# One adaLN row by ScalarE and accumulating transfers, and the sums over later keys as products of high and low parts

## The chip, the cores and the metric

One Trainium2 chip, one of its NeuronCores. The time is device microseconds of one execution of the whole kernel, as the median of several runs; lower is better. The engines are PE (TensorE, the matrix unit; PEld is its loading of weights), DVE (VectorE), ACT (ScalarE), POOL (GpSimd, which also issues transfers) and SP (SyncE, which issues transfers only). Each engine works through its own list of instructions in order; semaphores hold an instruction until what it needs is there.

## The reference

One layer of a decoder, in float32: batch 1, 512 positions, width 2048. The part that the change touches:

```python
c_act = jax.nn.silu(c)
mod = c_act @ w_ada[layer] + b_ada[layer]          # 2048 x 12288
sh1, sc1, gt1, sh2, sc2, gt2 = jnp.split(mod[:, None, :], 6, axis=-1)
h = rmsnorm(x, g_mix[layer]) * (1 + sc1) + sh1
x = x + (1 + gt1) * mixer(h, positions, w_in[layer], w_a[layer], w_b[layer], w_o[layer])
...
# stick-breaking attention, 8 heads of 128, in blocks of 128 queries
z = jnp.einsum('bqhd,bkhd->bhqk', q_blk, k) * scale
log1m = jnp.where(past, -jax.nn.softplus(z), 0.0)
after = lax.cumsum(log1m, axis=3, reverse=True) - log1m
w = jnp.where(past, jnp.exp(jax.nn.log_sigmoid(z) + after), 0.0)
```

`gt1`, the mixing gate's row, is a product of one vector with a 2048 x 2048 part of `w_ada`. `after` is, for each query and key, the sum of `log1m` over the later keys. The mixer has a second group of 8 heads, sparse ones, whose keys are chosen by an indexer: 16 small heads score every key, and the 256 best stay.

## The kernel before, in words

**High and low parts.** Most products take float32 operands as two fp32r numbers each, a high part (a copy by ACT, L168) and a low part (the difference, by DVE, L170), and three matmuls: high by high, high by low, low by high (`mm3`, L178 to L180). PE takes such a matmul in one pass. Products with plain f32 operands are exact and take two passes.

**Stages.** Up to 190 us: the norm, the first adaLN rows, queries of the indexer. From 190 to 800 us 31 calls of `unit`, each a pair of 128-column blocks of the input projection; beside each one the function `between` is called twice, and each call moves a piece of other work one step on (`work`: rope tables, the indexer's ropes, the shift's values) and may do one adaLN product. From 829 to 877 us the index loop: PE makes the dots (L905), ACT the relu (L907), DVE weighs and adds them (L912), three blocks for each of 16 index heads; ropes are split before by L896 and L897. Then the eight stick-breaking heads (to about 985 us), beside which DVE picks the best 256 of the scores (L932, L933); the eight sparse heads (to 1115 us); the projections `w_b` and `w_o`; the up-projection (1400 to 2240 us) and the down-projection.

**Fills.** `values(0)` and `values(1)` project the values of the sparse heads, 32 steps of six matmuls of 512 columns each (L178 to L180 on banks `att`). The index loop and the heads call `run(fill, n)` to set such steps between their own work, so that PE has something to do while a score goes through ACT and DVE. The order in which an engine at last has its instructions is not the order of the code: a scheduler sets it when the kernel is built.

**A stick-breaking head.** `stick_1`: scale q (L964), the scores z (L971, L972), absolute value, exp, ln (L975 to L978, ACT). `stick_2`: the softplus, masked (L985, DVE), and sums of its strips, `a` and `b` (L989 to L991). `stick_3`: nine products with a triangle or with ones add the sums over later keys onto z in PSUM (L1003), then exp (L1007). `stick_4`: the weights by the values (L1013), one head late.

**The adaLN rows.** The six rows of `mod` are 96 tiles of 128 numbers. For `w_ada` lying transposed, one number is the dot of a row of the tile with c. Such a tile is two halves of 128 x 1024: a load of 512 KB (`ada_load`, L576 and the loop above) and one instruction of DVE that multiplies and adds up along the row (L585, `some_ada`), which ends in a read of its sum. Tiles 32 to 79, 96 halves, are spread over the units, the index loop, the stick-breaking and the sparse heads; `ada_end(32, 48)` finishes the mixing gate's tiles, and `ts` adds 1. The last gate's row is made otherwise, beside the up-projection: ACT scales 128 x 1024 of `w_ada` by c (L1397), and a transfer adds the product to a DRAM tile (L1398).

**Transfers.** `fetch`, `save` and `queries` issue on POOL (L838, L875), `load` and `ada_load` on SP. A transfer with `accum_op` adds to what lies in DRAM.

## Time and profile before

| | us |
|---|---|
| median of 3 runs | 2684.82 |
| fastest and slowest of them | 2680.04, 2685.26 |
| the profiled execution | 2685.6 |
| its span | 2683.8 |
| adaLN products on DVE (L585, 91 recorded) | 109.4 |
| index loop (first L886 to first scores, L971) | 829.3 to 876.5 |
| first L1003 of heads 0, 1, ..., 7 | 883.63, 897.14, ..., 974.00 |

The span runs from the first to the last instruction of the profiled execution, all else of its time lies around it. In a row of the timeline stand the start, the duration, the engine, the line and operation, what is written from what, and its shape; a row with x8 is eight instructions that follow each other, and its duration is that of the group. In brackets stands how long the engine was idle before it, and what it waited for. A matmul's duration holds its latency too, so that its price in a sequence is the distance from its start to the next start. The DMA share is the mean busy share of the 16 DMA engines.

### The profile page before, as it was taken

Reading aid. Unit: us, or ns where it says so; the run is one execution under the profiler, and the core shown is the slowest. Engines: PE = TensorE matmul, PEld = TensorE weight load, DVE = VectorE, ACT = ScalarE, POOL = GpSimd, SP = SyncE. Lnnn points to the kernel's source line nnn. Section 1 sums busy time; section 2 is a strip of 40 time slices with the busy share of each in tenths; the row PEclk is TensorE's granted clock in tenths of the full one; section 3 lists DMA queues with packets and bytes.
Section 4 is the critical chain, followed back from the end, with each engine's and each line's share of the span. In section 5 each row is a group of like instructions: output and inputs, shape, how many; then the busy total and the mean of one; then the engine's idle time right before and its main releaser. Section 6 shows DMA issues by size and latency. Waiting matters only on the chain.

```text
span 2683.8 us, 47520 instructions
## 1 busy us (share of the span) xinstructions
PE 2653.4 (99%) x18644; PEld 2430.8 (91%) x18644; DVE 2396.1 (89%) x3395; ACT 1436.1 (54%) x2031; POOL 322.6 (12%) x526
## 2 busy tenths in 40 slices
PE   8999999999999999999999999999999999999998
PEld 6779999999997778889999999999999998887877
DVE  8979989999988999889888999999999997888887
ACT  4445455554446665435565555555555555546443
POOL 0010011000012211112220000000000001003121
PEclk9999999999999999999999999999999999999999
DMA  9984565566676638856763366666666646559775
GB/s 352 346 298 138 174 212 189 189 204 227 205 218 224 223 127 281 298 183 207 233 201 108 128 186 188 185 181 181 178 185 177 183 137 236 166 164 246 213 227 150
DMA packets 166157, 546.40 MB, mean 204 GB/s; under 512 B 21718, under 2 KB 22358, under 8 KB 165932
## 3 DMA queue, kind: packets, MB, share of 16 engines
q1 hardware_dynamic: 117804, 402.72, 45.6%
q0 software_dynamic: 47536, 140.26, 18.8%
q8 instruction: 146, 2.39, 0.3%
q14 instruction: 79, 0.65, 0.1%
q10 hardware_dynamic: 592, 0.39, 0.0%
HBM read 451.35 MB, written 88.52 MB: 201 GB/s over the span
## 4 chain that ended last, share of the span: by engine, by line
PE 87%; DVE 5%; DMA 3%; issue 2%; ACT 2%; POOL 0%; SPq 0%; ACTq 0%; POOLq 0%; DVEq 0%
PE att L179 14%; PE att L178 14%; PE att L180 14%; PE acc L179 13%; PE acc L180 13%; PE acc L178 12%; DVE wl L170 1%; DMA raw<-in_w_qi 1%; PE acc L1003 1%; DMA sumd<-F 1%; PE outs L179 1%; PE outs L178 1%; PE outs L180 1%; PE outs L1110 1%; ACT wh L168 1%
## 5 line engine op out<-in xcount | busy, mean ns | idle before, releaser
L168 ACT ACTIVATE wh<-raw 128x1024 fp32r<-128x1024 f32 (+2 forms) x783 | 822.3, 1056 | 936.2 <-DVE raw L295 188.4
L170 DVE TENSOR_TENSOR wl<-raw,wh 128x1024 fp32r<-128x1024 f32 (+2 forms) x783 | 945.0, 1214 | 121.0 <-ACT wh L168 113.8
L178 PE MATMUL acc<-F,wh 128*128 128x256 f32 (+3 forms) x2427 | 692.4, 286 | 1.8 <-ACT F L512 1.1
L180 PE MATMUL acc<-F,wl 128*128 128x256 f32 (+3 forms) x2427 | 690.0, 284 | 2.8 <-DVE wl L170 2.7
L179 PE MATMUL acc<-F,wh 128*128 128x256 f32 (+3 forms) x2427 | 689.8, 284 | 0.3 <-DVE F L540 0.3
L178 PE MATMUL att<-F,wh 128*128 128x256 f32 (+2 forms) x2420 | 688.8, 285 | 0.1
L180 PE MATMUL att<-F,wl 128*128 128x256 f32 (+2 forms) x2420 | 687.2, 284 | 0.0
L179 PE MATMUL att<-F,wh 128*128 128x256 f32 (+2 forms) x2420 | 686.6, 284 | 0.2 <-DVE F L199 0.2
L178 PEld LDWEIGHTS acc<-F,wh 128*128 128x128 f32 (+1 forms) x2427 | 454.8, 187 | 14.1 <-ACT wh L168 3.6
L180 PEld LDWEIGHTS acc<-F,wl 128*128 128x128 f32 (+1 forms) x2427 | 454.8, 187 | 11.1 <-DVE wl L170 4.1
L179 PEld LDWEIGHTS acc<-F,wh 128*128 128x128 f32 (+1 forms) x2427 | 455.0, 188 | 8.0 <-DVE F L540 0.5
L178 PEld LDWEIGHTS att<-F,wh 128*128 128x128 f32 x2420 | 454.3, 188 | 8.3 <-ACT wh L168 1.7
L179 PEld LDWEIGHTS att<-F,wh 128*128 128x128 f32 x2420 | 454.4, 188 | 6.3 <-DVE F L199 0.7
L180 PEld LDWEIGHTS att<-F,wl 128*128 128x128 f32 x2420 | 454.3, 188 | 6.2 <-DVE wl L170 0.6
L178 PE MATMUL att<-wh,F 128*128 128x512 f32 x448 | 178.9, 400 | 0.2 <-ACT wh L168 0.2
L179 PE MATMUL att<-wl,F 128*128 128x512 f32 x448 | 175.0, 391 | 0.0
L180 PE MATMUL att<-wh,F 128*128 128x512 f32 x448 | 174.6, 390 | 0.0
L179 PE MATMUL acc<-wl,F 128*128 128x512 f32 x288 | 114.2, 397 | 2.7 <-DVE wl L170 2.7
L178 PE MATMUL acc<-wh,F 128*128 128x512 f32 x288 | 113.0, 394 | 2.3 <-ACT wh L168 2.3
L180 PE MATMUL acc<-wh,F 128*128 128x512 f32 x288 | 111.9, 393 | 0.0
L585 DVE SCALAR_TENSOR_TENSOR raw<-raw,raw 128x1024 f32<-128x1024 f32 x91 | 109.4, 1217 | 0.0
L178 PEld LDWEIGHTS att<-wh,F 128*128 128x128 f32 x448 | 84.3, 188 | 20.2 <-issue 2.0
(404 smaller groups left out, 3773.2 us busy)
## 6 DMA issues: line engine op xcount, KB each, us to landing
raw<-in_w_up SPq DMA_DIRECT2D x164, 512.0 KB, 3.6
raw<-in_w_ada SPq DMA_DIRECT2D x154, 512.0 KB, 5.5
raw<-in_w_x SPq DMA_DIRECT2D x128, 512.0 KB, 4.4
raw<-in_w_down SPq DMA_DIRECT2D x98, 512.0 KB, 4.4
xd<-F POOLq DMA_DIRECT2D x64, 256.0 KB, 2.9
F<-xd POOLq DMA_DIRECT2D x64, 256.0 KB, 4.6
raw<-in_w_o SPq DMA_DIRECT2D x32, 512.0 KB, 4.4
soft<-in_w_gate SPq DMA_DIRECT2D x32, 512.0 KB, 3.7
```

Source lines behind the costliest of these rows:

```text
L168: pins["wh"] = act(wh, raw, AF.Copy)
L170: pins["wl"] = tt(wl, raw, wh.bitcast(F32), ALU.subtract)
L178: mm(ps, ah, bh, start=first, stop=False, skip_group_check=not check)
L179: mm(ps, ah, bl, start=False, stop=False, skip_group_check=not check)
L180: return mm(ps, al, bh, start=False, stop=last, skip_group_check=not check)
L585: stt(w, w, 1.0, cb[half], ALU.mult, ALU.mult, accum_out=macc[:, t, half : half + 1])
L1003: mm(o, negtri if tri else negones, i, start=False, stop=True, skip_group_check=True)
L1110: mm(o[:, b * P : (b + 1) * P], vs[kb][:, hd % 4 * HD : (hd % 4 + 1) * HD], pT[b][:, kb * P : (kb + 1) * P], start=kb == 0, stop=kb == b)
```

## The change

Three parts. **First**, the row of the mixing gate, `mod[:, 32:48]`. It leaves `ada_left`, so 32 of 96 products on DVE go. A generator `mix_gate` makes it instead: 64 times SP loads 128 x 512 of `w_mix`, the gate's part of `w_ada` as it lies, ACT multiplies it with a column of c, and POOL issues a transfer that adds it to one of four DRAM tiles `mix0` to `mix3`. Four rounds fold the 128 rows of each of these to 64, 32, 16 and 8 by a load of the upper half and an accumulating store onto the lower one, four of each a round; at last one matmul with a 0/1 matrix `pick` adds up the remaining rows and puts the 2048 numbers where `mod` has them. One step of the generator runs with each call of `between`, eight in the index loop, two with each stick-breaking head until it ends.

**Second**, in the stick-breaking heads, the softplus is split into a high part (three copies on ACT) and a low part (three subtractions on DVE). Seven of the nine products of `stick_3`, those on the softplus itself, become two fp32r matmuls each, high and low, with fp32r copies of the triangle and of ones (`exact`). The two products on `a` and `b` stay f32.

**Third**, the fills and the remaining adaLN products are spread anew: the index loop takes 24 steps of `fill` in place of 32, what is left goes to the heads, and adaLN products stand only beside the units and the sparse heads.

```diff
--- before.py
+++ after.py
@@ -561,7 +561,7 @@
         save(qid[j][:, LATE], o[:, LATE])
 
 
-    ada_left = [(t, half) for half in range(2) for t in range(32, 80)]
+    ada_left = [(t, half) for half in range(2) for t in range(48, 80)]
     cb[1] = None
 
     ada_ready = []
@@ -802,6 +802,45 @@
                 ada_soft.append((w, t, half))
             yield
 
+    mix_sum = [dr.tile([P, S], F32, tag=f"mix{b}", name=f"mix{b}") for b in range(4)]
+
+    def mix_gate():
+
+        ahead = None
+        for n in range(4 * KT + 1):
+            if ahead:
+                k, b, w = ahead
+                act(w, w, AF.Copy, scale=c_col[:, k : k + 1])
+                save(mix_sum[b], w, **({"accum_op": ALU.add} if k else {}))
+            if n < 4 * KT:
+                k, b = divmod(n, 4)
+                w = slot()
+                nc.sync.dma_start(w, A["w_mix"][k, :, b * S : (b + 1) * S])
+                ahead = k, b, w
+            yield
+        for rows in (64, 32, 16, 8):
+            parts_ = []
+            for s in mix_sum:
+                t = slot()[:, : 4 * rows]
+                save(t, s[rows : 2 * rows].rearrange("r (h c) -> (r h) c", c=4 * rows))
+                parts_.append(t)
+            yield
+            for s, t in zip(mix_sum, parts_):
+                save(s[:rows].rearrange("r (h c) -> (r h) c", c=4 * rows), t, accum_op=ALU.add)
+            yield
+        x, pick = slot()[:, :P], slot()[:, :KT]
+        save(pick, A["pick"])
+        for b, s in enumerate(mix_sum):
+            save(x[32 * b : 32 * b + 32], s[:8].rearrange("r (j f) -> (r j) f", f=P))
+        yield
+        yield
+        ps = outs()
+        mm(ps[:, :KT], x, pick, start=True, stop=True)
+        stt(mod[:, 32:48], ps[:, :KT], 1.0, b_ada[:, 32:48], ALU.add, ALU.add)
+        yield
+
+    mix = mix_gate()
+    next(mix)
     shift = shift_values()
 
     def beside():
@@ -818,6 +857,7 @@
                 ada_load()
             with behind(*pins):
                 next(work)
+                next(mix)
                 if i:
                     some_ada()
 
@@ -945,14 +985,10 @@
     run(index)
     fill = values(0, vb[0])
     for i in range(16):
-        run(fill, 2)
-        last = run(index, 2 if i == 15 else 1)
+        run(fill, 1 if i % 2 else 2)
+        run(index, 2 if i == 15 else 1)
         if i % 2:
-            with behind(*([last] if last else [])):
-                some_ada(len(ada_ready))
-        else:
-            ada_load()
-    run(fill)
+            run(mix)
 
 
     with behind(sig):
@@ -989,18 +1025,26 @@
         tt(a, two[:, P:], one, ALU.add)
         tt(b[:, :P], three[:, P : 2 * P], two[:, :P], ALU.add)
         tt(b[:, P:], three[:, 2 * P :], a, ALU.add)
-        return (a, b), last
+        hi = t2k("ta", 2, F32R), t2k("ta", 2, F32R), t2k("sp", 2, F32R)[:, : 2 * P]
+        lo = slot(F32R), slot(F32R), slot(F32R)[:, : 2 * P]
+        for n in (1, 2, 0):
+            sp = of_soft(soft)[n]
+            act(hi[n], sp, AF.Copy)
+            last = tt(lo[n], sp, hi[n].bitcast(F32), ALU.subtract)
+        return (a, b, strips(*hi), strips(*lo)), last
 
     def stick_3(zs, soft, later):
-        a, b = later
-        one, two, three, four = strips(*of_soft(soft))
+        a, b, hi, lo = later
+        one, two, three, four = zip(hi, lo)
         z1, z2, z3, z4 = strips(*zs)
         for o, i, tri in (
-            (z3, three, True), (z1, one, True), (z3[:, P : 2 * P], two[:, :P], False), (z3[:, 2 * P :], a, False),
+            (z3, three, True), (z1, one, True), (z3[:, P : 2 * P], cols(two, 0), False), (z3[:, 2 * P :], (a,), False),
             (z2, two, True), (z2[:, P:], one, False),
-            (z4, four, True), (z4[:, P : 2 * P], three[:, :P], False), (z4[:, 2 * P :], b, False),
+            (z4, four, True), (z4[:, P : 2 * P], cols(three, 0), False), (z4[:, 2 * P :], (b,), False),
         ):
-            mm(o, negtri if tri else negones, i, start=False, stop=True, skip_group_check=True)
+            w = negtri if tri else negones
+            for t in i:
+                mm(o, exact[:, tri * P : tri * P + P] if len(i) > 1 else w, t, start=False, stop=True, skip_group_check=True)
         w = t2k("w", 2), t2k("w", 2), t2k("sp", 2)
         for n in (1, 2, 0):
             W = (S, S, 2 * P)[n]
@@ -1017,9 +1061,15 @@
             save(yad[hd], ya[hd])
             ya[hd] = None
 
+    exact = slot(F32R)[:, : 2 * P]
+    act(exact, const[:, 2:4].rearrange("p a c -> p (a c)"), AF.Copy)
+    def both_values(first=fill):
+        yield from first
+        yield from values(1, vb[1])
+
     yad = dram("yad", 4)
     ya = [None] * NH
-    fill = values(1, vb[1])
+    fill = both_values()
     va = [fetch(vd[b]) for b in range(NQB)]
     before = None
     fetched = {}
@@ -1038,7 +1088,6 @@
 
     td = dram("td", KT)
     for hd in range(NH):
-        ada_load((3, 3, 2, 2, 3, 0, 0, 0)[hd])
         state = stick_1(hd)
         if hd + 1 < NH:
             pairs.append([fetch(xd[2 * hd + 2]), fetch(xd[2 * hd + 3])])
@@ -1046,17 +1095,17 @@
             stick_4(*before, va)
             if hd % 4 == 0:
                 va = [fetch(vd[hd + b]) for b in range(NQB)]
-        run(fill, 1 if hd < 4 else 2)
+        run(fill, 2)
+        run(mix, 2)
         if hd == NH - 1:
             cosT, sinT = (fetch(rope_d[0][:, i * S : (i + 1) * S]) for i in range(2))
             fetch_pair(0)
             for i in range(4):
                 ya[i] = fetch(yad[i])
         later, last = stick_2(*state)
-        run(fill)
+        run(fill, 1 if hd < 4 else 2)
         with behind(last):
             run(index, 3)
-            some_ada(len(ada_ready))
         before = hd, stick_3(*state, later)
         run(fill)
     run(index, 100)
@@ -1139,20 +1188,18 @@
         run(fill)
         with behind(last):
             some_ada(2 if hd > 1 else 0)
-        ada_load(2 if hd else 0)
+        ada_load()
         last = sparse_2(p, s)
         run(fill)
-        if hd > 5:
-            ada_load(3)
+        if hd > 3:
+            ada_load()
         before = hd, sparse_3(p), vb[hd // 4]
         with behind(last):
-            some_ada((2 if hd else 0) + (3 if hd > 5 else 0))
+            some_ada(2 if hd > 3 else 1)
         run(fill, 2)
     y[:3] = [split(o) for o in y[:3]]
     sparse_4(*before, y)
     run(fill)
-    ada_end(32, 48)
-    ts(mod[:, 32:48], mod[:, 32:48], 1.0, None, ALU.add)
 
 
     y[3:] = [split(o) for o in y[3:]]
@@ -1752,6 +1799,9 @@
     ada = i["w_ada"][0]
     a["w_ada"] = asc(ada[:, : 5 * D].T)
     a["w_gate"] = asc(ada[:, 5 * D :]).reshape(KT, P, D)
+    a["w_mix"] = asc(ada[:, 2 * D : 3 * D]).reshape(KT, P, D)
+    q, j = np.arange(P)[:, None], np.arange(KT)[None, :]
+    a["pick"] = asc(((q // 32 == j // 4) & (q % 4 == j % 4)).astype(np.float32))
     a["b_gate"] = asc(i["b_ada"][0][5 * D :]).reshape(1, D)
     a["c_col"] = asc(i["c"][0].reshape(KT, P).T)
 
```

PE has 18287 rows in the change and 18222 before, DVE 3173 and 3183, ACT 2079 and 1990, POOL 632 and 531, SP 854 and 822. Lines after the change have other numbers: L905 is L945, L907 is L947, L964 is L1000, L971 is L1007, L1003 is L1047, L1013 is L1057, L838 is L878, L875 is L915.

PE before, stick-breaking head 1, from its last scores on: L971 and L972 are scores and mask, L1013 the weights of head 0 by values, L178 to L180 a fill, L1003 the sums of head 1.

```order
L971 MATMUL acc_9730<-F_9623,F_9625 128x512
L972 LDWEIGHTS mask_71
L972 MATMUL acc_9730<-mask_77,mask_71 128x128
L1013 MATMUL outs_9751<-w_9710,F_9577 128x384
L1013 MATMUL outs_9751<-sp_9711,F_9579 128x256
L1013 MATMUL outs_9751<-w_9709,F_9575 128x512
L178 MATMUL att_9627<-wh_79,F_1152 128x512
L179 MATMUL att_9627<-wl_83,F_1152 128x512
L180 MATMUL att_9627<-wh_79,F_1153 128x512
```

Two more such triples follow, for banks att_9628 and att_9629, and then the sums. In the change the same place reads (L1007 and L1008 scores and mask, L1057 weights by values, L1047 the sums; `ta` and `sp` are high parts, F_10011 a low part, F_9779 the copies `exact`):

```order
L1007 MATMUL acc_9952<-F_9827,F_9829 128x512
L1008 LDWEIGHTS mask_71
L1008 MATMUL acc_9952<-mask_77,mask_71 128x128
L1057 MATMUL outs_9973<-w_9940,F_9791 128x128
L1057 MATMUL outs_9973<-w_9940,F_9787 128x384
L1057 MATMUL outs_9973<-sp_9941,F_9789 128x256
L1057 MATMUL outs_9973<-w_9939,F_9785 128x512
L1047 MATMUL acc_9953<-ta_10008,F_9779 128x384
L1047 MATMUL acc_9954<-sp_10009,F_9779 128x256
L1047 MATMUL acc_9952<-ta_10007,F_9779 128x512
L1047 MATMUL acc_9953<-F_10011,F_9779 128x384
```

The nine fill matmuls between the weights by values and the sums have gone from head 1; they stand earlier or later. In head 0 seven stand where there were 20, and from head 2 on 18 or 24 stand in this place.

POOL before, at the index loop: L875 loads the queries of index heads, two at a time, from `index`; L838 loads head 0's q and k (xd_1609, xd_1610).

```order
L875 DMA F_9187<-index_1900 128x384
L875 DMA F_9262<-index_1901 128x384
L875 DMA F_9337<-index_1902 128x384
L875 DMA F_9412<-index_1903 128x384
L838 DMA F_9567<-xd_1609 128x512
L838 DMA F_9569<-xd_1610 128x512
```

POOL in the change, from the load of the last pair of index heads' queries back to the fold before it and on to head 0's q: L825 is a fold's load, L829 its accumulating store, on tiles mix_1905 to mix_1908; L915 loads queries, L878 head 0's q.

```order
L829 DMA mix_1905<-F_9540 128x128
L829 DMA mix_1906<-F_9542 128x128
L829 DMA mix_1907<-F_9544 128x128
L829 DMA mix_1908<-F_9546 128x128
L915 DMA F_9630<-index_1903 128x384
L825 DMA F_9684<-mix_1905 128x64
L825 DMA F_9686<-mix_1906 128x64
L825 DMA F_9688<-mix_1907 128x64
L825 DMA F_9690<-mix_1908 128x64
L829 DMA mix_1905<-F_9684 128x64
L829 DMA mix_1906<-F_9686 128x64
L878 DMA F_9775<-xd_1609 128x512
```

Loads that stood next to each other now stand behind folds of the row, which wait for the folds before them.

ACT in the change, in the index loop: L936 splits queries, L947 is the relu, L1065 makes `exact`, L1000 scales head 0's q.

```order
L947 ACTIVATE w_9531<-acc_9528 128x384
L936 ACTIVATE F_9728<-F_9630 64x384
L936 ACTIVATE F_9731<-F_9630 64x384
L947 ACTIVATE w_9537<-acc_9534 128x512
L947 ACTIVATE w_9569<-acc_9566 128x256
L1065 ACTIVATE F_9779<-const 128x256
L947 ACTIVATE w_9575<-acc_9572 128x384
L947 ACTIVATE w_9581<-acc_9578 128x512
L1000 ACTIVATE F_9775<-F_9775 128x512
L947 ACTIVATE w_9599<-acc_9596 128x256
```

The scaling of q, which needs POOL's last row above, stands behind the relus of nine of the sixteen index heads and ahead of the others.

## Prediction

> **What bounds the kernel now.** I read the page from the top: span, busy shares, then the chain.
>
> ```profile
> span 2683.8 us, 47520 instructions
> PE 2653.4 (99%) x18644; PEld 2430.8 (91%) x18644; DVE 2396.1 (89%) x3395; ACT 1436.1 (54%) x2031; POOL 322.6 (12%) x526
> PE 87%; DVE 5%; DMA 3%; issue 2%; ACT 2%; POOL 0%; SPq 0%; ACTq 0%; POOLq 0%; DVEq 0%
> ```
>
> PE is busy 99% of the span and carries 87% of the chain, so a matmul that goes is worth its column time wherever PE is the limit. VectorE's 89% is a mean over stages. The windows view splits it (busy us of PE, PEld, DVE, ACT, POOL with instruction counts; granted clock; DMA share; GB/s): the units, the index loop, the stick-breaking heads, the sparse heads, the up-projection.
>
> ```profile
> 190.00:800.00 610.00, 609.24 (x5244) 602.56 (x5243) 564.99 (x728) 314.28 (x423) 55.28 (x97) 1.00 0.60 192
> 829.30:876.50 47.20, 46.81 (x212) 35.17 (x212) 44.00 (x77) 33.55 (x68) 5.90 (x11) 1.00 0.60 199
> 883.00:990.00 107.00, 106.69 (x476) 75.91 (x474) 100.72 (x240) 66.07 (x99) 19.38 (x36) 1.00 0.56 190
> 1030.00:1115.00 85.00, 85.00 (x444) 70.55 (x443) 78.40 (x170) 41.20 (x87) 14.49 (x27) 1.00 0.84 293
> 1400.00:2240.00 840.00, 839.98 (x7213) 829.56 (x7213) 783.00 (x960) 481.98 (x632) 56.71 (x85) 1.00 0.59 170
> ```
>
> PE has no gap in the units and in the up-projection. In the index loop VectorE is at 44.0 of 47.2 us, and PE's matmuls wait for what it frees. In the heads VectorE is at 94%.
>
> **The products of the sums: -7.3 us of PE.** The timeline of PE in head 5 (start, duration, line) gives every price by start-to-start.
>
> ```profile
> 946.10 0.39 PE L179 MATMUL att<-wl,F 128*128 128x512 f32 x1
> 946.32 0.39 PE L180 MATMUL att<-wh,F 128*128 128x512 f32 x1
> 946.55 1.25 PE L1003 MATMUL acc<-soft,const 128*128 128x384 f32 x6
> 947.64 0.39 PE L1003 MATMUL acc<-T,const 128*128 128x128 f32 x2
> 947.86 1.90 PE L1003 MATMUL acc<-soft,const 128*128 128x256 f32 x8
> 949.60 0.60 PE L1003 MATMUL acc<-T,const 128*128 128x256 f32 x2
> 949.84 0.58 PE L178 MATMUL att<-wh,F 128*128 128x512 f32 x1
> 950.26 0.40 PE L179 MATMUL att<-wl,F 128*128 128x512 f32 x1
> ```
>
> A high/low (fp32r) matmul of 512 columns takes 0.227 us (946.32 to 946.55); in the up-projection 839.98 / 7213 = 0.116 us is the mean of mostly 256 columns. An exact f32 product has two rows, two passes: two of 128 columns take 947.64 to 947.86, 0.11 each; the other rows resolve into 0.217, 0.322 and 0.43 a pass for 256, 384 and 512. The seven products on the softplus are four of 128 columns and one each of 384, 256 and 512. As a high and a low matmul the last three cost 2 x 0.17, 2 x 0.113 (three quarters and half of 0.227) and 2 x 0.227 instead of 2 x 0.322, 2 x 0.217, 2 x 0.43: 0.30 + 0.21 + 0.40 = 0.91 us a head, **7.3** for eight. For fp32r at 128 columns no row exists. One end is 0.057, a quarter of 0.227 (4 x 2 x 0.053 = 0.42 a head, 3.4 in all, so 10.7); the other is 0.116, a whole one of 256 (0.4 lost, so 6.9). I take 0.11, the exact pass, since loading 128 columns of weights comes with either.
>
> The Trainium skill, "TensorE: Matmul & The Clock Gate", section Back-to-back issue gap, gives about 81 ns sustained for N=128. By it the sum would be about -9.2; the two-pass rows at 110 ns don't show it, and its section LDWEIGHTS (columns / 1.2 ns, 107 ns for 128) agrees with them.
>
> **What makes high and low.** Three copies on ScalarE and three subtractions on VectorE now stand between the softplus and its sums. These rows are head 0's chain: first score, last score's end, ln, the masking on VectorE, the first sum; then the same start and end in head 1; then what PE waited for at the sums.
>
> ```profile
> 876.48 0.81 PE L971 MATMUL acc<-F,F 128*128 128x384 f32 x2
> 879.00 0.48 PE L178 MATMUL att<-wh,F 128*128 128x512 f32 x1
> 879.23 0.60 ACT L975 ACTIVATE soft<-acc 128x512 f32<-128x512 f32 x1 [0.59 <-PE acc L972]
> 881.55 1.26 ACT L978 ACTIVATE soft<-soft 128x1280 f32<-128x1280 f32 x1
> 882.85 1.62 DVE L985 SCALAR_TENSOR_TENSOR soft<-acc,soft 128x512 f32<-128x512 f32 x3 [3.31 <-ACT soft L978]
> 884.78 0.28 DVE L991 TENSOR_TENSOR T<-soft,T 128x128 f32<-128x128 f32 x1
> 883.63 1.76 PE L1003 MATMUL acc<-soft,const 128*128 128x384 f32 x8
> 890.09 0.83 PE L971 MATMUL acc<-F,F 128*128 128x384 f32 x2
> 894.54 0.80 PE L178 MATMUL att<-wh,F 128*128 128x512 f32 x1
> 895.17 0.39 PE L179 MATMUL att<-wl,F 128*128 128x512 f32 x1
> 897.14 0.91 PE L1003 MATMUL acc<-soft,const 128*128 128x384 f32 x2
>   DVE soft L985: 1.4, 4
> ```
>
> Scores to sums take 7.15 and 7.05 us, and PE has 2.5 us of scores to do in that time; the rest is fills (20 in head 0; in head 1 the last head's weights by values, to about 894.94, then 9). After the change the first high part is there at about 7.6 (first masking 0.6, copy 0.6, as L975's row) and the first low part at 9.2 (behind the additions that end at 885.06, 0.69 more, the price of a 512-wide masking). The order of the change puts 7 fills there in head 0, none in head 1, and in head 2 eighteen that need four evacuations which ScalarE has queued behind the ln. So PE is idle: head 0, 7.6 - (2.5 + 1.6) = 3.5, and 1.0 more for the low parts: 4.5; head 1, 7.6 - 4.85 + 1.0 = 3.8; head 2, evacuated at 7.1 (ln's end 6.3, plus rest): 2.3. Together 10.6, less the 1.4 that PE waits at all sums now: **+9.2** (ends: 0 if the fills slide in, 10.6). Heads 3 to 7 have 4.85 us of work and 18 or 24 fills (4.1 or 5.4) in that place against 9.2, so the six new instructions are hidden; uncovered they'd cost 2.1 a head. VectorE's 1.5 us more per head (as L985's three) is paid by the adaLN products that leave.
>
> **Fills move.** Counted in the two orders: 9 more before the index loop (+2.0 us), 25 fewer within it, 22 more between the first scores and the last sums (+5.0), 6 fewer later (-1.4). The 25 are worth nothing by themselves, as VectorE sets that loop.
>
> **The index loop.** VectorE loses six adaLN products there, and ScalarE waits for other things:
>
> ```profile
> L585 DVE SCALAR_TENSOR_TENSOR raw<-raw,raw 128x1024 f32<-128x1024 f32 x6 | 7.3, 1219 | 0.0
> 832.15 1.74 ACT L907 ACTIVATE w<-acc 128x256 f32<-128x256 f32 x4 [0.68 <-issue]
> 858.92 0.92 ACT L907 ACTIVATE w<-acc 128x512 f32<-128x512 f32 x2 [1.05 <-DVE F L912]
> L875 POOL DMA_DIRECT2D F<-index x8: 536/536/557, 824.3 to 829.6; - x8
> DMA to landing us min/median/max: 2.5/5.6/6.5
> L1447 POOL DMA_DIRECT2D sumd<-F x40: 858/900/3281, 2337.8 to 2551.7; - x40
> DMA to landing us min/median/max: 3.9/8.4/18.5
> DMA to landing us min/median/max: 5.2/8.1/9.1
> ```
>
> (The landing rows are those of the query transfers, of sumd's accumulating stores of 256 KB, and of the gate's, 512 KB.) Before, all eight query loads were issued by 829.63; T0 is the loop's start, 829.30. In the change loads 4 to 7 and head 0's q and k stand in POOL's order between folding rounds, each of which waits for the round before to land. The last accumulating store of the row goes at T0+4.5 (behind the first relus, 832.15). Then q follows three landings in sequence; two rounds between them cost 4.6 each (0.5 for the query load, 0.5 for the last fold load, four issues of 0.9 by L1447's row), and 2.8 of issues plus 2.5 to land come behind: q is there at T0 + 19 + 3 x La. ScalarE scales q behind the ninth of sixteen index heads, in place before at 858.92, T0+29.6, and without the four products of 1.22 ahead of it at T0+24.7. ScalarE is in order, so relus, scores and VectorE stop behind it. La is no shorter than 3.9 by the rows and up to 8.1; I take **4.2**, near the least, since these stores are 256 KB and smaller. q lands at T0+31.6, a stall of 6.9. Without it the scores of head 0 would start 7.3 earlier; so -7.3 + 6.9 = **-0.4** (ends: -7.3 with no stall; +11.3 with La 8.1).
>
> The Trainium skill, "DMA: Bandwidth & Descriptors", section Anatomy of one DMA, gives a fixed cost of about 2.0 us; by it La is little over 2, q is there at about T0+25, and there is no stall. The least accumulating landing here is 3.9, so the trace speaks against it for this kind.
>
> **The adaLN row.** ScalarE gets 64 copies of 512 columns with a column as scale, SyncE 64 loads of 256 KB, POOL 64 accumulating stores, nearly all in the units.
>
> ```profile
> L451 ACT ACTIVATE F<-F,amp x16: 721/725/727, 11.5 to 90.7; 128x512 fp32r<-128x512 f32 x16
> L1397 ACT ACTIVATE soft<-soft,c_col x32: 1137/1142/1148, 1548.1 to 2139.4; 128x1024 f32<-128x1024 f32 x32
> ```
>
> 62 x 0.73 = 45 us on ScalarE's 314 of 610, with DMA at 0.60. I cost it at nothing: the same pattern (L1397 and its stores) runs in the up-projection at 482 of 840 and 0.59, and PE is busy 839.98 of 840 there. If a quarter of the copies delayed a split that PE waits for, it would be +11. VectorE has 8 products fewer in the sparse heads (9.8 us); PE is busy 85.00 of 85 there, so I take **-0.5** (ends 0 and -2). The single matmul that picks the row, and the end of the old row that goes, are under 0.3.
>
> **Sum**: 2.0 - 0.4 + 5.0 - 1.4 + 9.2 - 7.3 - 0.5 = **+6.6** on the profiled execution's 2685.6, that is 0.8 above the median; against the median 2684.8 it is **2691**.
>
> **Rivals.** *In time*: the folding is quick, q lands before T0+24.7, that is La below 1.9 us. Then the index loop gives its 7.3 and the sum is -0.3: 2684.5. For it: the stores are small, and the best plain landing is 2.5. Against: no accumulating one under 3.9. *PE is the limit throughout* (the other side): PE is at 99%, fills slide into the holes of heads 0 to 2, and what is left is -7.3 and -0.5: 2677, and 2674 if 128 columns are cheap. It decides if low parts arrive within 5 us of the scores, or fills stand there after all; 7.05 us before the new copies speaks against it. *Long folding*: La at the rows' median 8.1, +11.3 in place of -0.4, so +18.3: 2703. For it: 5.2 is the least of the 512 KB stores. *Units pay*: +11 and the rest, 2702; the 609.24 of 610 in the units leaves no slack, the up-projection speaks against it. That the change *doesn't save what it says*, because a matmul of 512 columns isn't at 0.227, is excluded by the rows from 946.10 on.
>
> **Chances.** Forecast 0.42 (2685 to 2696), in time 0.21, PE the limit 0.14, long folding 0.18, units 0.05. A measurement tells about 0.2%, 5.4 us: 2679.5 to 2690.2 is the same. Faster: PE the limit, and the lower edge of in time, 0.16. The same: the rest of in time, 0.19, and 0.18 of the forecast: 0.37. Slower: 0.24 of the forecast, long folding, units: 0.47. The range 2676 to 2703 leaves out about half of long folding and most of units on top, and a third of PE the limit below: under 0.2.
>
> **What would show it.** Right: sums at 2.56 us instead of 3.48 a head; PE idle 3 to 5 us ahead of the sums in heads 0 and 1; ScalarE waiting for a transfer at the q scaling or a query load in the index loop; units unchanged. Wrong: POOL's folding loads land before ScalarE gets there, scores of head 0 start 40 us after T0, no idle PE in the heads, or the units longer than 610 us. The forecast falls if La is under 2 or over 8, or if the fills cover the sums.

## The result, and the profile after

| | before | after |
|---|---|---|
| median, us | 2683.41 (4 runs, 2680.04 to 2685.26) | 2713.16 (4 runs, 2711.62 to 2715.41) |
| ratio of the runs | | 1.011, 95% interval 1.0097 to 1.0123 |
| profiled span | 2683.8 | 2709.9 |

Slower by 30 us; forecast were 2691 and a range of 2676 to 2703. The way was right, the size was not. These are two of the page's lines after the change, and the granted clock of PE in 40 slices of the span (in tenths, so a 9 is 90% or more).

```profile
span 2709.9 us, 47944 instructions
PE 2661.4 (98%) x18646; PEld 2440.1 (90%) x18646; DVE 2376.2 (88%) x3353; ACT 1487.4 (55%) x2120; POOL 403.6 (15%) x627
PEclk9999999999999899999999999999999999999999
```

PE's busy share hides it, but the clock line has an 8, and that slice is 881 to 949 us, where the index loop ends and the heads begin. The windows view of the change, for the units, the way to the index loop, the loop (835.9 to 884.0), heads 0 to 2, heads 3 to 7:

```profile
190.00:800.00 610.00, 606.71 (x5204) 599.81 (x5203) 558.21 (x718) 347.36 (x478) 108.11 (x157) 1.00 0.82 243
800.00:835.90 35.90, 35.37 (x216) 30.88 (x214) 20.55 (x26) 19.29 (x26) 9.65 (x16) 1.00 0.88 268
835.90:884.00 48.10, 43.02 (x186) 32.97 (x186) 37.58 (x64) 32.92 (x67) 30.74 (x48) 0.93 0.73 173
884.00:932.30 48.30, 38.33 (x147) 27.05 (x147) 30.55 (x84) 29.21 (x48) 8.12 (x17) 0.82 0.20 57
932.30:1002.00 69.70, 69.70 (x336) 53.75 (x335) 58.08 (x130) 45.80 (x70) 14.37 (x27) 1.00 0.44 148
```

And the heads of before, 0 to 2 and 3 to 7:

```profile
876.50:911.20 34.70, 34.70 (x159) 24.20 (x159) 29.44 (x72) 23.10 (x36) 5.55 (x10) 1.00 0.66 213
911.20:977.50 66.30, 66.20 (x300) 47.81 (x299) 61.74 (x149) 38.07 (x56) 13.83 (x26) 1.00 0.59 202
```

The 26.1 us of the two spans lie as follows: 6.6 until the loop starts (829.3 to 835.9), 0.9 in the loop (47.2 to 48.1), **13.6 in heads 0 to 2** (34.7 to 48.3, with 12 matmuls fewer), 3.4 in heads 3 to 7, which hold 36 matmuls more, and 1.6 behind. In heads 0 to 2 PE idles for 10 us of 48, and the granted clock is 0.82 in the mean of the whole stage, which is worth 8.7 us of its 48.3 at most. Finer windows of the change show how one follows from the other: the idle time of head 0, its sums, then head 1 from its scores to its sums, and its sums.

```profile
888.30:892.30 4.00, 0.19 (x2) 0.00 (x1) 2.57 (x4) 3.24 (x5) 0.00 (x0) 0.98 0.13 15
892.30:897.90 5.60, 5.58 (x20) 4.79 (x20) 2.36 (x7) 1.99 (x5) 0.00 (x0) 0.50 0.22 83
901.10:908.60 7.50, 5.03 (x20) 2.80 (x20) 4.79 (x15) 6.23 (x9) 1.37 (x3) 1.00 0.02 3
908.60:914.90 6.30, 5.52 (x18) 4.49 (x19) 6.09 (x18) 2.59 (x5) 3.15 (x6) 0.55 0.42 137
```

After 4 us without work PE runs at a clock of 0.50 for the next 5.6 us. The sums, which take 2.4 us in heads 3 to 6, take those 5.6 in head 0. The timeline says what PE waited for (the last row is head 1's first sum):

```profile
888.10 0.39 PE L180 MATMUL att<-wh,F 128*128 128x512 f32 x1
892.30 0.69 PE L1047 MATMUL acc<-ta,F 128*128 128x384 f32 x1 [3.81 <-ACT ta L1032]
908.63 0.44 PE L1047 MATMUL acc<-ta,F 128*128 128x384 f32 x1 [2.46 <-ACT ta L1032]
```

In head 0 it is the high part, 8.3 us behind the first score. This is the hole that was foreseen (3.5 us); what followed it was not. The Trainium skill, "TensorE: Matmul & The Clock Gate", section What's actually happening, has this rule: after an idle window of some 3.4 us the clock falls to half, and as long a busy one brings it back. The rows of head 0 agree. The hole of head 1 is shorter than that window, 2.46 us, and the clock was 0.55 behind it all the same, so the length of a hole does not decide alone. The trace of before shows the same near its end, where it could have been read ahead of the prediction: PE idles for 2.31 us, and then the clock is 0.50 for 6.8 us.

```profile
2607.84 0.49 PE L178 MATMUL acc<-wh,F 128*128 128x512 f32 x1 [2.31 <-ACT wh L168]
2608.20:2615.00 6.80, 6.03 (x15) 4.65 (x15) 6.80 (x9) 3.68 (x6) 3.26 (x6) 0.50 0.86 230
```

In the index loop the same stands once more, on a smaller scale. ACT waits for a query load, PE for ACT, and the clock is halved behind it:

```profile
857.17 1.05 ACT L936 ACTIVATE F<-F 64x384 fp32r<-64x384 f32 x2 [4.17 <-DMA F<-index]
858.68 0.80 PE L945 MATMUL acc<-F,F 128*128 128x256 f32 x2 [4.13 <-ACT w L947]
858.70:864.70 6.00, 6.00 (x17) 5.13 (x18) 5.15 (x9) 3.63 (x8) 4.79 (x8) 0.50 0.78 121
870.81 0.63 ACT L1000 ACTIVATE F<-F 128x512 f32<-128x512 f32 x1 [0.97 <-DMA F<-xd]
```

And in the units PE's longest wait is at one place. It waits 1.53 us there for a weight copy of ScalarE (L168), which stands behind a copy of the row (L813) and behind a wait of 1.46 us for a buffer that a store of rope values still holds. VectorE waits 2.67 us for a buffer that an accumulating store of the row holds, but that wait ends before the copy comes: its next split (L170) waits for ScalarE.

```profile
344.75 0.64 ACT L697 ACTIVATE F<-w 32x512 f32<-32x512 f32 x1 [1.46 <-DMA rope<-F]
346.58 0.72 ACT L813 ACTIVATE F<-F,c_col 128x512 f32<-128x512 f32 x1
347.20 2.94 ACT L168 ACTIVATE wh<-raw 128x1024 fp32r<-128x1024 f32 x3
347.18 0.43 DVE L332 TENSOR_TENSOR F<-sp,ta 128x256 f32<-128x256 f32 x1 [2.67 <-DMA mix<-F]
348.28 2.36 DVE L170 TENSOR_TENSOR wl<-raw,wh 128x1024 fp32r<-128x1024 f32 x2 [0.67 <-ACT wh L168]
348.30 0.39 PE L178 MATMUL att<-F,wh 128*128 128x256 f32 x1 [1.53 <-ACT wh L168]
```

In the 20 us around it PE has 140 matmuls where it had 179 before (first row before, second after). At the 0.116 us that one takes on average in the up-projection, these 39 are 4.5 us.

```profile
340.00:360.00 20.00, 20.00 (x179) 20.00 (x178) 16.60 (x21) 14.86 (x23) 2.15 (x4) 1.00 0.57 200
340.00:360.00 20.00, 17.71 (x140) 17.31 (x139) 13.57 (x16) 11.74 (x17) 3.98 (x6) 0.91 0.80 222
```

To tell idle time from slow time I took, for each PE matmul, the distance to the next start, less the time its columns take at full clock (0.227 us per 512 columns of fp32r, 0.43 per pass of f32; the loss). A table of this stands with the experiments.

### The profile page after: what moved, and what is told of

It reads as the page before. It is cut to its first block, busy times and chain, and to the rows that moved or that the text cites. A ratio compares the mean times of both kernels' runs of the same rounds, so it can differ in the third digit from the quotient of the medians.

```text
span 2709.9 us, 47944 instructions
## 1 busy us (share of the span) xinstructions
PE 2661.4 (98%) x18646; PEld 2440.1 (90%) x18646; DVE 2376.2 (88%) x3353; ACT 1487.4 (55%) x2120; POOL 403.6 (15%) x627
## 4 chain that ended last, share of the span: by engine, by line
PE 56%; DVE 3%; DMA 2%; issue 1%; ACT 1%; POOL 0%; ACTq 0%; POOLq 0%; DVEq 0%
PE att L180 8%; PE acc L179 8%; PE att L178 8%; PE att L179 8%; PE acc L180 8%; PE acc L178 8%; DVE wl L170 1%; DMA raw<-in_w_down 1%; PE outs L1159 1%; PE acc L1128 1%; PE outs L180 1%; PE outs L179 1%; PE outs L178 1%; PE acc L1362 0%; DMA sumd<-F 0%
## 5 line engine op out<-in xcount | busy, mean ns | idle before, releaser
L168 ACT ACTIVATE wh<-raw 128x1024 fp32r<-128x1024 f32 (+2 forms) x783 | 821.6, 1055 | 908.5 <-DVE raw L295 184.9
L170 DVE TENSOR_TENSOR wl<-raw,wh 128x1024 fp32r<-128x1024 f32 (+2 forms) x783 | 945.2, 1215 | 128.0 <-ACT wh L168 120.0
L178 PE MATMUL acc<-F,wh 128*128 128x256 f32 (+3 forms) x2427 | 692.8, 286 | 1.5 <-ACT F L512 0.7
L178 PE MATMUL att<-F,wh 128*128 128x256 f32 (+2 forms) x2420 | 690.0, 285 | 3.2 <-ACT wh L168 1.5
L180 PE MATMUL acc<-F,wl 128*128 128x256 f32 (+3 forms) x2427 | 690.1, 284 | 2.0 <-DVE wl L170 1.9
L180 PE MATMUL att<-F,wl 128*128 128x256 f32 (+2 forms) x2420 | 688.4, 285 | 1.2 <-DVE wl L170 1.1
L178 PEld LDWEIGHTS acc<-F,wh 128*128 128x128 f32 (+1 forms) x2427 | 454.8, 187 | 13.0 <-ACT wh L168 2.6
L178 PEld LDWEIGHTS att<-F,wh 128*128 128x128 f32 x2420 | 455.0, 188 | 12.3 <-ACT wh L168 3.5
L180 PEld LDWEIGHTS acc<-F,wl 128*128 128x128 f32 (+1 forms) x2427 | 454.8, 187 | 10.1 <-DVE wl L170 3.3
L180 PEld LDWEIGHTS att<-F,wl 128*128 128x128 f32 x2420 | 455.1, 188 | 8.0 <-DVE wl L170 2.6
L178 PE MATMUL att<-wh,F 128*128 128x512 f32 x448 | 179.4, 401 | 0.9 <-DVE F L337 0.5
L180 PE MATMUL att<-wh,F 128*128 128x512 f32 x448 | 175.8, 393 | 0.0
L178 PE MATMUL acc<-wh,F 128*128 128x512 f32 x288 | 113.1, 394 | 1.4 <-ACT wh L168 1.4
L180 PE MATMUL acc<-wh,F 128*128 128x512 f32 x288 | 111.9, 393 | 0.0
L178 PEld LDWEIGHTS att<-wh,F 128*128 128x128 f32 x448 | 85.2, 190 | 20.7 <-issue 1.2
L179 PEld LDWEIGHTS att<-wl,F 128*128 128x128 f32 x448 | 84.8, 189 | 18.4 <-issue 1.2
```

The source lines that it names most:

```text
L168: pins["wh"] = act(wh, raw, AF.Copy)
L170: pins["wl"] = tt(wl, raw, wh.bitcast(F32), ALU.subtract)
L178: mm(ps, ah, bh, start=first, stop=False, skip_group_check=not check)
L179: mm(ps, ah, bl, start=False, stop=False, skip_group_check=not check)
L180: return mm(ps, al, bh, start=False, stop=last, skip_group_check=not check)
```

## The parts apart

Four kernels: high and low parts alone, the adaLN row alone, the change with the old fills, the change with the folding elsewhere.

**hilo_only**: before, with the new `stick_3`, its copies and subtractions.

> The kernel before with the high and low products alone (three copies, three subtractions a head, seven of nine sums as fp32r pairs); fills and adaLN row as before. Theory A (the change lost its time to idle PE in heads 0 to 2, because its fills are elsewhere, and to the lower clock that follows): the split chain is covered by the 20 or more fills that stay in each head, PE is idle no longer than before, the sums take 2.4 us in place of 3.5: about 8 us faster, 2675. Rival B (the split itself lengthens each head's chain beyond its cover): 2 us a head lost, no faster than before or slower, 2684 to 2692.

Measured 2696.31, ratio 1.0046 (1.0031 to 1.0061). Theory A fell here. With all of before's fills kept, the high and low parts cost 11 us. VectorE, busy for 91.2 us of the heads' 101 before, has 103.9 of 115 now (three subtractions a head, 14.2 us in all), and the scheduler put only 12 to 17 fills ahead of the sums of heads 2 to 6, and 4 in head 7:

```profile
878.60:993.80 115.20, 106.82 (x486) 77.34 (x486) 103.93 (x243) 74.70 (x118) 19.01 (x36) 0.97 0.56 189
PE acc L1011 <- ACT ta L996: 6.7, 7, 3.0
```

(The second line is from the waits: 6.7 us in all, 7 times, the longest 3.0.)

**mix_only**: before with `mix_gate`, without the products it replaces, and with the change's places for the adaLN products that stay.

> The kernel before with the adaLN row by ScalarE and accumulating transfers alone, folding in the index loop as in the change; sums and fills as before. Theory A: the folding holds up the query loads in the index loop (a hole of about 4 us and a lower clock behind it, +6), the stores hold buffers in the units (+5), heads 0 to 2 keep their fills and have no holes: 2691 to 2696. Rival C (all of the change's loss comes from the folding, through late loads of q and k): holes in heads 0 to 2 here too, 2705 or more. Rival D (VectorE's relief outweighs it): 2680 or less.

Measured 2696.48, ratio 1.0047 (1.0031 to 1.0064), at the edge of theory A. Heads 0 to 2 have no holes (C falls); VectorE has no adaLN product left in the loop and the heads, where 20 are recorded before, and it brings nothing (D falls). That fits PE, which was busy for 34.70 of 34.70 and 66.20 of 66.30 us of the heads before. In the units VectorE waits 4.2 us for a buffer that a store of the row holds, and PE 1.7 us for the split behind it. The loop's start is at 837.1 in place of 829.3, and the loop takes 48.0 in place of 47.2.

**fills_back**: the change with this:

```diff
-        run(fill, 1 if i % 2 else 2)
+        run(fill, 2)
...
+    run(fill)
...
-    fill = both_values()
+    fill = values(1, vb[1])
...
-        run(fill, 2)
+        run(fill, 1 if hd < 4 else 2)
...
-        run(fill, 1 if hd < 4 else 2)
+        run(fill)
```

> The change with the fills as they were before (two steps in each pass of the index loop, the rest of the first values behind it, the second values beside the heads). Theory A: the holes of heads 0 to 2 and the clock behind them go (20 us), the folding's hole in the index loop stays: 2688 to 2695. Rival B or C: the holes stay with other fills, 2705 or more.

Measured 2699.11, ratio 1.0055 (1.004 to 1.007): 14 us of the change's 30 are the new place of the fills, less than theory A had. The loss in heads 0 to 2 falls from 22.5 us to 4.6.

**folds_late**: `run(mix)` taken from the index loop and the heads and set into the sparse heads.

> The change with the four folding rounds and the pick moved from the index loop and the first heads to the sparse heads; fills as in the change. Theory A: no wait for a query load in the index loop, scores of head 0 start 41 to 44 us after the loop's start in place of 48, but heads 0 to 2 keep their holes and the low clock: 2703 to 2708. Rival C: the holes go with the folding, 2685 or less.

Measured 2706.24, ratio 1.0084 (1.0069 to 1.0099): 7 us of the 30 are the folding in the loop. The scores of head 0 start 40.9 us after the loop does, as VectorE's own pace had it; the holes stay (C falls).

PE's loss in us, with what its stage lasts in brackets, by the sums described above:

| | index loop | heads 0 to 2 | heads 3 to 7 | 53 us behind |
|---|---|---|---|---|
| before | 5.5 (47.2) | 1.9 (34.6) | 2.4 (66.3) | 2.1 |
| hilo_only | 7.0 (48.7) | 6.0 (43.5) | 16.1 (71.7) | 4.3 |
| mix_only | 8.8 (48.0) | 2.5 (35.8) | 2.0 (65.9) | 2.1 |
| fills_back | 9.5 (49.9) | 4.6 (39.5) | 8.2 (63.7) | 9.4 |
| folds_late | 4.4 (40.9) | 25.2 (50.4) | 4.0 (69.6) | 5.9 |
| after | 12.1 (48.1) | 22.5 (48.3) | 4.0 (69.6) | 5.9 |

In heads 0 to 2 of the change, 12.0 of the 22.5 is what starts come later than 2.2 times the column time; this is idle time. The other 10.5 is starts that are late by less than that. Of these the clock can explain 8.7 at most, by its mean of 0.82 over 48.3 us; the rest is waits too short for the mark.

## The clock, and the fills

**warm** tests the clock by itself: matmuls that nobody reads, in the idle time.

```diff
+    WARM = (32, 24, 20)
...
+        if hd < 3:
+            ps = outs()
+            with behind(scores[hd]):
+                for _ in range(WARM[hd]):
+                    mm(ps[:, : 2 * P], exact[:, :P], exact, start=True, stop=True)
```

> The change with 32, 24 and 20 matmuls of 256 columns that nothing reads, set into the idle time of heads 0, 1 and 2 behind their scores (8.6 us of PE work more). Theory A, the clock: the granted clock stays near 1.0 in heads 0 to 2, the sums of heads 0 and 1 take under 4 us in place of 5.6 and 5.9, the scores of head 3 start 6 to 10 us earlier after those of head 0 (48 before): 2703 to 2708 in spite of more work. Rival E (the sums of heads 0 and 1 are long because each waits for its low part, the clock is beside the point): no gain, 2712 to 2722.

Measured 2707.85, ratio 1.0077 (1.0062 to 1.0092), so 5 us faster than the change with more work. Heads 0 and 1 take 14.4 and 12.3 us in place of 17.1 and 13.8. Head 2 takes 2.2 more, as its matmuls came in front of its fills. Windows of warm, head 0 from its scores on and from its sums on:

```profile
885.20:892.70 7.50, 7.50 (x50) 6.03 (x49) 3.22 (x7) 5.79 (x9) 1.21 (x3) 1.00 0.30 74
892.70:899.60 6.90, 5.57 (x29) 3.73 (x28) 4.66 (x11) 4.33 (x9) 0.58 (x2) 1.00 0.23 76
```

The clock is 1.00 where it was 0.50, and the sums take 3.9 us in place of 5.6 (4.4 in head 1, in place of 5.9, where under 4 was expected), though fills and a product of the index stand between those of head 0 now. That doing useless work makes heads 0 and 1 shorter is what theory E can't have: the low parts alone did not make them long. The predicted 6 to 10 us from head 0 to head 3 became 2 (46.3 in place of 48.3), because of head 2.

**pinned** holds each head's fills behind its scores (`with behind(scores[hd]):` around the three `run(fill, ...)`), which gives heads 0 and 1 the 24 that the code writes there. **pinned_late** has that and the folding in the sparse heads.

> The change with each head's fills held behind its own scores, so that the 41 fill matmuls that had moved into the index loop stay in heads 0 and 1. Theory A: heads 0 to 2 lose 3 to 5 us in place of 22, and hold 9.3 us more work, the index loop keeps its 48 us as PE doesn't set it: 2702 to 2706. Rival E (waits for the low parts, whatever stands there): no gain, 2711 or more.

> Both at once, fills held behind the scores and the folding moved to the sparse heads. Theory A: the two causes lie in different stages and add: 7 us for the folding and 9 for the fills, 2695 to 2700. If the folding's stall only gave way to VectorE's own pace with fewer fills beside it, 2703 or more.

Measured 2706.42, ratio 1.0078 (1.0063 to 1.0093), and 2699.01, ratio 1.0048 (1.0033 to 1.0063), the first at the upper edge of theory A, the second within it. The two causes lie apart and add. Heads 0 to 2 still lose 9.3 us: head 2 waits for the evacuations, as predicted.

**hilo_spread**: hilo_only with the fills pinned and all ahead of the sums, and the heads' adaLN products of VectorE moved behind the sparse heads.

```diff
+        with behind(scores[hd]):
+            run(fill, (5, 3, 3, 3, 3, 3, 4, 4)[hd])
...
```

> The kernel before with the high and low sums, fills held behind the scores and all ahead of the sums (30 in head 0, 18 in 1 to 5, 24 in 6 and 7), and the stick-breaking heads' adaLN products moved behind the sparse heads. Theory A with the split chain of 9 us: covered in every head, the 8 us of PE work are kept: 2676 to 2681. Rival B (the split can't be covered): 2685 or more.

Measured 2707.1, ratio 1.0074 (1.0058 to 1.0091). It failed twice over. The products that moved cost 11 us at w_o (PE loses 17.8 us there in place of 6.6). And PE loses 9.3 us in the 40 us that begin 13 us behind the last sums, which the next kernels show without the first.

## Everything covered, and still no gain

**combo** is fills_back with folding in the sparse heads and the fills as in hilo_spread. **combo_exact** is the same with the old sums. **combo_raw** lets the row's tiles go through the ring of weight buffers:

```diff
-                w = slot()
+                w = t2k("raw", 8, w=1024)[:, :S]
```

> The change with three things put right: folding in the sparse heads, 32 steps of fills in the index loop as before, and each head's fills behind its scores and ahead of its sums (30 in head 0, 18 in 1 to 5, 24 in 6 and 7). Theory A (three separate causes: uncovered heads with the clock behind them, the folding's stall, buffers held by the stores in the units): the first two go, the units' 6 us stay, high and low parts bring their 8 less some waits: 2680 to 2687. Rival F (high and low parts bring nothing here even when covered, since a head's chain grows by the 2 us of the split): 2688 to 2692, as combo_exact.

> As combo with the sums as before, exact f32 without high and low parts. Theory A: 5 to 8 us slower than combo. Rival F: equal within 2 us, or faster.

> As combo, and the row's 64 tiles go through the ring of weight buffers instead of the shared ring F, so that no store holds a buffer that VectorE waits for in the units. Theory A: the units' loss of 5 us (index loop starts at 836 to 837 in place of 829) goes to 1, 3 to 5 us faster than combo. Rival G (ScalarE's copies or the transfers' share delay the units): as combo.

combo 2699.69, ratio 1.005 (1.0033 to 1.0067); combo_exact 2690.58, ratio 1.0021 (1.0012 to 1.0031); combo_raw 2834.87, ratio 1.0553 (1.0531 to 1.0576). The last is a failure that says nothing of theory A or G: the loads of weights then wait for buffers that stores hold, and VectorE waits 104 us for them in the units. No run took away what the units lose through the row (6.6 us in the profile of the change). The wait shown above is about 4.5 us of it, and why ScalarE comes late there was not tested.

So what fills_back and folds_late save does not add here: without 14 and 7 us the change would be at 2692. Rival F held, and by more: covered in every head, high and low parts cost 9 us. The heads do get shorter (103.4 us from first scores to last sums, combo_exact 106.0). But VectorE still has the top-k to end, which the first sparse heads wait for. Its last step ends 18.3 us behind the last sums in combo, 13.5 in combo_exact, and PE has used up its fills as cover. In the 40 us that begin 13 us behind the last sums, its matmuls have 30.4 us of column time in combo and 39.2 in combo_exact. It is busy there for 34.62 us in combo (first row) and 39.95 in combo_exact:

```profile
999.80:1039.80 40.00, 34.62 (x164) 26.46 (x164) 36.70 (x83) 20.83 (x45) 14.28 (x24) 0.96 0.65 184
1000.00:1040.00 40.00, 39.95 (x209) 32.92 (x208) 39.45 (x88) 26.29 (x57) 16.39 (x27) 1.00 0.73 229
```

VectorE's rows of combo there, with the top-k (L972, L973) between the splits of the outputs (L199) that PE waits for:

```profile
1000.44 0.68 DVE L972 MAX8 m<-F 128x8 f32<-128x512 f32 x1
1001.05 0.67 DVE L199 TENSOR_TENSOR F<-F,F 128x512 fp32r<-128x512 f32 x1
1001.64 0.08 DVE L973 MATCH_VALUE_LOAD F<-m,F 128x8 f32 x1
1001.71 0.67 DVE L973 MATCH_REPLACE8 F<-m,F 128x512 f32<-128x512 f32 x1
1002.30 0.68 DVE L199 TENSOR_TENSOR F<-F,F 128x512 fp32r<-128x512 f32 x1
...
1009.82 1.22 DVE L170 TENSOR_TENSOR wl<-raw,wh 128x1024 fp32r<-128x1024 f32 x1
```

and what PE had to wait for:

```profile
1003.04 0.51 PE L179 MATMUL att<-F,wh 128*128 128x512 f32 x1 [0.30 <-DVE F L199]
1011.09 0.79 PE L180 MATMUL att<-F,wl 128*128 128x512 f32 x1 [3.21 <-DVE wl L170]
```

**combo_topk, exact_topk, before_topk** test that: `run(index, 4)` in place of `run(index, 3)`, so that the top-k ends beside the heads.

> As combo, with four steps of the top-k beside each stick-breaking head in place of three, so that none is left behind the last head. Theory H (the high and low parts lose what they bring since VectorE's 14 us of subtractions push the top-k behind the heads, where the first sparse head waits for it and PE has no fills left): PE loses 1 to 3 us in the 53 us behind the last sums in place of 11, 2690 to 2694. Theory B (the split's chain in each head): no gain, 2698 or more.

> As combo_exact with the same four steps of the top-k. Theory H: there the last top-k is covered by fills that the heads left, so next to nothing: 2688 to 2692. With it and combo_topk, what high and low parts are worth once the top-k is out of the way: theory H has them equal or combo_topk up to 5 us ahead, theory B has exact sums ahead by 6 or more.

> The kernel before with four steps of the top-k beside each head. VectorE is at 94% there already: 2683 to 2690, no better than before.

combo_topk 2705.93, ratio 1.0076 (1.0059 to 1.0093); exact_topk 2692.38, ratio 1.0025 (1.0015 to 1.0036); before_topk 2686.9, ratio 1.0006 (0.9997 to 1.0016). In combo_topk PE loses 0.5 us in those 40 us in place of 9.6, as theory H had it. But the heads grow from 103.4 to 118.5 us, since the low parts now stand behind the top-k in VectorE's list:

```profile
PE acc L1049 <- DVE F L1035: 7.9, 5, 2.5
883.00:987.00 104.00, 92.92 (x409) 67.98 (x410) 89.14 (x221) 63.57 (x100) 17.89 (x34) 0.94 0.31 103
```

The total is what theory B said, the 40 us behind are what theory H said, so neither holds alone. The work of VectorE is paid in the heads or behind them, wherever it is put. Exact sums do not mind either place. No kernel tried beats the one before.

## Why the prediction came out wrong

The spans differ by 26.1 us where +6.6 was forecast. With the terms of the forecast laid on the stages (a matmul of 512 columns at 0.227 us, a head's sums at -0.91), heads 0 to 2 were to cost 3.8 and cost 13.6; the way to the loop 2.0 and 6.6; the loop -0.4 and 0.9; heads 3 to 7 3.6 and 3.4; all that follows -1.9 and 1.6.

**High and low parts on PE, -7.3**: right, but for heads 0 and 1, whose sums took 5.6 and 5.9 us, at a clock of 0.50 and 0.55. From the sums' first start to their last it is 3.27 us before (946.55 to 949.82) and 2.38 after in heads 3 to 6, 0.89 a head where 0.91 was forecast. At 128 columns the starts are 0.05 to 0.12 apart, 0.09 on average in head 4, under the 0.11 that was taken; starts behind an exact product are a little later than supposed, and it is luck that the two cancel. The Trainium skill, "TensorE: Matmul & The Clock Gate", section Back-to-back issue gap, gives 81 ns for 128 columns; the trace lies a little above it.

**The index loop, -0.4**: right in size, +0.9. An accumulating store of a fold landed in 3.5 us in the median, where 4.2 was taken, and in 2.4 at best, so 3.9 was no floor. q was scaled 34.9 us after the loop's start where it was forecast to land at 31.6. Without the folds the loop takes 40.9 us (folds_late), so the stall is worth 7.2 where 6.9 was forecast. But ACT lost most at a query load, 4.2 us, and 1 us at q, both behind the same stores, and PE ran 6.0 us at half the clock behind that, which was not forecast. So the size is partly luck.

```profile
L829 POOL DMA_DIRECT2D mix<-F x16: 899/1422/1959, 847.9 to 882.4; - x16
DMA to landing us min/median/max: 2.4/3.5/7.1
```

**The holes of heads 0 to 2, +9.2**: this step failed, and it is the largest part of the miss. The idle time was sized well (10.6 forecast, 12.0 measured). But it was priced as idle time only, with PE at full clock behind it. The rest of the loss there is 10.5 us, and the half clock is up to 8.7 of it; warm, which keeps the clock at 1.00 ahead of the sums of head 0 and through them, shows that it is worth time. The step "PE is idle: head 0 ... 4.5; head 1 ... 3.8; head 2 ... 2.3. Together 10.6, less the 1.4" should have been about twice that (a loss of 22.5 us, where before had 1.9).

**The units, at nothing, and 2.0 before the loop**: failed. The loop starts 6.6 us late, not 2.0. The start moves between executions: 825.5 to 831.8 in the four profiled kernels without the row, 829.1 in the mean, and 835.9 to 841.6 in eleven with it (combo_raw left out), 837.6 in the mean. So what the change costs there is nearer 8.5 than 6.6. The pattern of the up-projection was taken as proof, yet there the stores hold buffers of another ring. What stands in ScalarE's list ahead of a weight copy, and whose buffers the stores keep until they land, was not asked. How much of the price either has stays open.

**VectorE's 1.5 us a head, "paid by the adaLN products that leave"**: right in the heads (88.6 us of 118), wrong behind them. The top-k ended 18.8 us behind the last sums in place of 14.9, and with it the forecast -1.4 and -0.5 for later fills and the sparse heads became +1.6.

**The other rivals.** Long folding did not come; the range's top was built on it, so it did not reach the case that came. Units pay, held at 0.05, came in part: a weight copy was late behind a copy of the row, at one place and for 4.5 us in place of 11.

## What to carry to other kernels

The idle holes of PE in heads 0 to 2, 10 us together, cost up to 8.7 us more here through the clock behind them; the granted clock of a single stage is the place to look first. A saving on PE that was bought with work of VectorE was worth nothing where VectorE was next in line, and where that is has to be asked of the stage behind, too. Before a transfer takes over work, ask which buffers it holds until it lands, and what stands behind it in its queue.

## What was not expected of the hardware

The half clock is sharp. In the timeline of the change's index loop, behind the wait of 4.1 us, matmuls of 512 columns start 0.42 us apart, and from 865.56 on 0.23 again:

```profile
862.48 0.63 PE L180 MATMUL att<-wh,F 128*128 128x512 f32 x1
862.90 0.63 PE L178 MATMUL att<-wh,F 128*128 128x512 f32 x1
...
865.56 0.40 PE L179 MATMUL att<-wl,F 128*128 128x512 f32 x1
865.79 0.39 PE L180 MATMUL att<-wh,F 128*128 128x512 f32 x1
```

In combo a wait of 1.9 us is enough for a mean clock of 0.74 in the 6.6 us behind it, while two waits of 0.6 and 0.85 us have 1.00 around and behind them:

```profile
881.00:883.40 2.40, 0.52 (x2) 0.09 (x1) 2.28 (x4) 2.38 (x5) 0.00 (x0) 1.00 0.00 0
883.40:890.00 6.60, 6.56 (x22) 4.19 (x23) 1.06 (x2) 3.40 (x6) 0.00 (x0) 0.74 0.24 79
940.00:947.00 7.00, 5.54 (x27) 4.24 (x26) 6.47 (x16) 3.92 (x6) 5.19 (x10) 1.00 0.48 169
947.00:953.00 6.00, 6.00 (x33) 4.27 (x32) 5.69 (x16) 4.43 (x8) 3.28 (x7) 1.00 0.99 372
```

(The first window holds the wait, the third the two.) An accumulating store of 128 KB or less lands in 2.4 us at best and 3.5 in the median (L829 above), near the 2.5 us of the quickest plain load of queries before; the row's stores of 256 KB in the units, with a DMA share of 0.82, took 7.1 in the median.
